# First FFN of a two-layer decoder: product in PSUM, table preparation in finer steps, first table loads issued by GpSimd

## The chip, the cores and the metric

The kernel runs on one core of a Trainium2 chip. The metric is device time in microseconds (us) of one execution. The engines are TensorE (PE, matrix products), VectorE (DVE), ScalarE (ACT), GpSimd (POOL) and SyncE (SP, which issues most DMAs). Each engine works through its own instructions in order and waits on semaphores for the others. SBUF is the on-chip memory; PSUM holds the results of PE in eight banks of 128 x 512 fp32.

## The reference

Two layers over x of 512 positions by 1024 channels, fp32: layer 0 has an attention mixer, layer 1 a diagonal state-space mixer (S5), and each is followed by the same kind of FFN. What the change touches is the FFN of layer 0 and, run beside it, the preparation of tables for the state-space layer.

```python
def conv_ffn(h, w_up, conv_w, conv_b, w_down):
    up = h @ w_up
    up = lax.conv_general_dilated(
        up, conv_w[:, None, :], window_strides=(1,), padding=[(CONV_W - 1, 0)],
        dimension_numbers=('NWC', 'WIO', 'NWC'), feature_group_count=2 * D_FF) + conv_b
    gate, val = jnp.split(up, 2, axis=-1)
    return (jax.nn.silu(gate) * val) @ w_down
...
    lam = lax.complex(a_re.astype(jnp.float32), a_im.astype(jnp.float32))
    lam_bar = jnp.exp(lam * dt)
    b_bar = ((lam_bar - 1) / lam)[..., None] * b_mat
```

D_FF is 2816, CONV_W is 3.

## The kernel before, in words

Every fp32 product is made of three matmuls with split operands (high times high, high times low, low times high; `mm3`, lines 169 to 173). A weight block `w_r` is loaded by SP (line 161), ACT rounds it to its high part `w_h` (L163), and DVE subtracts to get the low part `w_l` (L164). Three raw blocks and five split ones fit at a time.

The FFN has 22 units of 128 gate and 128 value channels, in groups of 8, 8 and 6. A unit takes two up products (`up_i_0` gate, `up_i_1` value; 24 matmuls of 128x512 each, one PSUM bank each). `unit_out` then works on them: `conv` (ACT L457 reads the bank and writes `ca` in SBUF, two DVE steps L459 add the other taps), Silu of the gate (ACT L466, in place), the product `gm` (DVE L469), its high part `gH` (ACT L473) and low part `gL` (DVE L474). The up products of the next units run on PE meanwhile. After each group come eight down products `dn_g_m` over the group's `gH` and `gL`. The PSUM pool `mm` has six banks handed out in turn, `aux` has two. The FFN of layer 1 uses the same function.

Beside the first FFN runs `ssm_prep`, a generator that computes the tables ("maps") of the state-space layer: powers and factors (`pw`, `fr`, `fi`, `lf`) on DVE and POOL, a recursion `tb` on POOL that is stored to `sR`, and then eight blocks. A block loads `lam` (from `sL`), `bt` and `bc`, makes `bl` and `cl` by complex products on POOL (`cmul`, L870 to 875, and L1073 to 1078), has PE multiply `cl` with `bd` into the small bank `pk` (L1017, in `direct`), makes `kz` of it, and stores `sB`, `sC` and `sT` by SP. `ball` is a table of the same kind as `bt`, loaded once before the blocks.

The order: the generator is written in steps (`yield`). `pace(us)` is called with 11.0 after each unit and 5.4 after each down product and takes one step for each `PACE` us; what a step writes stands in each engine's queue between the FFN's own instructions. `follow` chains the FFN's instructions on an engine, `held` keeps a DMA in program order on SP. `wg` are weight rows of the conditioning layer, loaded by SP and reduced on DVE (L196) between the rest.

Of the kernel before, what the change touches and what calls it, by code (L numbers as in the profile page):

```python
# [16 lines left out]
P = 128  # L17
# [24 lines left out]
BGU = 2  # L42
PACE = 12.0
NHOLD = 2
# [46 lines left out]
def _trunk(ctx, tc, I, out, tap):  # L91
# [47 lines left out]
    def follow(eng, fn):  # L139
        with tc.issue_after(line[eng].ins) if eng in line else ExitStack():  # L140
            line[eng] = fn()
        return line[eng]
# [281 lines left out]
    def ffn(l, R, prep=None, last=None, hook=lambda: None):  # L424
# [4 lines left out]
        with ExitStack() as fc:  # L429
# [33 lines left out]
            def unit_out(i, j, pss, nxt=lambda: None):  # L463
                cg = conv(i, 0, pss[0])
                nxt()
                follow("S", lambda: S.activation(cg, cg, AF.Silu))  # L466
                cv = conv(i, 1, pss[1])
                m = fp.tile([P, T], F32, tag="gm", bufs=1, name="gm")
                follow("V", lambda: V.tensor_tensor(m, cg, cv, ALU.mult))  # L469
                nxt()  # L470
                gh = fp.tile([P, T], F32R, tag=f"gH{j}", name=f"gH{i}")
                gl = fp.tile([P, T], F32R, tag=f"gL{j}", name=f"gL{i}")
                follow("S", lambda: S.activation(gh, m, AF.Copy))  # L473
                follow("V", lambda: V.tensor_tensor(gl, m, gh.bitcast(F32), ALU.subtract))  # L474
                return gh, gl
# [389 lines left out]
    def ssm_prep(fc):  # L865
# [14 lines left out]
        def gen():  # L880
# [30 lines left out]
            expo(mag, ph)  # L911
            yield

            V.tensor_tensor(ph, aim, dt, ALU.mult)
# [43 lines left out]
            V.tensor_tensor(fi, fi, den, ALU.mult)  # L958
            yield

            lf = pt_.tile([P, 2, 8, NPAIR], F32, tag="lf", name="lf")
            lt1, lt2 = (pt_.tile([P, 8, NPAIR], F32, tag=g, name=g) for g in ("lt1", "lt2"))
            f0, f1 = (f.rearrange("p (o q) -> p o q", o=1).to_broadcast([P, 8, NPAIR]) for f in (fr, fi))
            cmul(lf[:, 0, ::-1, :], lf[:, 1, ::-1, :], pw[:, 0, :8, :], pw[:, 1, :8, :], f0, f1, lt1, lt2)
            yield

# [10 lines left out]
            for hb in range(2):  # L977
# [5 lines left out]
                for q in range(6):  # L983
                    n = 1 << q
                    e0, e1 = bcast(co[:, 3 + q, ps_], n), bcast(si[:, 3 + q, ps_], n)
                    cmul(tb[:, 0, :, n:2 * n], tb[:, 1, :, n:2 * n], tb[:, 0, :, :n], tb[:, 1, :, :n], e0, e1, tt[:, 0, :, :n], tt[:, 1, :, :n])
                    if q > 3:
                        yield
                    if hb == 0 and q == 4:
                        lf_out()  # L990
# [14 lines left out]
            for ri in range(2):  # L1005
                SP.dma_start(ball[:, ri].rearrange("p a b -> p (a b)"), I[("b_re", "b_im")[ri]])

            def v3(t):
                return t[:, :512].rearrange("p (q o) -> p q o", o=16)

            cmul(bb[:, 0], bb[:, 1], ball[:, 0], ball[:, 1], bcast(fr, 16), bcast(fi, 16), v3(t1), v3(t2))

            def direct(bi, bd, cl):
# [6 lines left out]
                V.scalar_tensor_tensor(kz[:, 112:128], delta, sm("d_skip", bi, 1), kz[:, 112:128], ALU.mult, ALU.add)  # L1020
                for j in range(8):
                    SP.dma_start(sT[bi].rearrange("(h j) g c -> j g h c", j=8)[j], kz[:, 112 - 16 * j:240 - 16 * j])

            def held(out, in_):
                tc.keep_in_program_order(SP.dma_start(out, in_))

            def load_bl(bi):
                lam = pb.tile([P, 2, 512], F32, tag="lam", name="lam")
                bt = pb.tile([P, 2, 512], F32, tag="bt", name="bt")
                cs = slice(bi * 512, (bi + 1) * 512)  # L1030
                for ri in range(2):
                    held(lam[:, ri, :], sL[ri, :, cs].rearrange("(o j) x -> o j x", o=1).to_broadcast([16, 8, 512]))
                    held(bt[:, ri, :], I[("b_reT", "b_imT")[ri]][:, cs].rearrange("h (o x) -> h o x", o=1).to_broadcast([16, 8, 512]))
                return lam, bt
# [10 lines left out]
            for bi in range(8):  # L1045
                qs = slice(bi * 4, bi * 4 + 4)
                if owe:
                    cl_out(bi - 1, owe[2])
                bc = pb.tile([P, 2, 4, 16], F32, tag="bc", name="bc")
                for ri in range(2):  # L1050
                    held(bc[:, ri].rearrange("p a b -> p (a b)"), I[("c_re", "c_im")[ri]][:, bi * 64:(bi + 1) * 64])
                bl = pb.tile([P, 2, 512], F32, tag="bl", name="bl")
                lam, bt = nxt
                cmul(bl[:, 0], bl[:, 1], lam[:, 0], lam[:, 1], bt[:, 0], bt[:, 1], t1[:, :512], t2[:, :512])
                yield
                held(sB[bi].rearrange("p r n -> p (r n)"), bl.rearrange("p r n -> p (r n)"))
                if bi < 7:
                    nxt = load_bl(bi + 1)
                if owe:
                    direct(*owe)  # L1060
                cl = pb.tile([P, 2, 4, 9, 16], F32, tag="cl", name="cl")

# [17 lines left out]
                for g2 in range(2):  # L1080
                    rr = slice(g2 * 64, g2 * 64 + 64)
                    E.tensor_copy(bd[rr, :, :, g2 * 16:g2 * 16 + 16], bb[rr, :, qs, :])
                owe = bi, bd, cl
                yield
            cl_out(7, owe[2])
            direct(*owe)
            tc2.close()

# [407 lines left out]
```

## Time and profile before

| | |
|---|---|
| time, median of 3 runs | 1196.93 us (1194.94 to 1197.47) |
| profiled execution | 1194.65 us, its span 1192.7 us, mean granted clock 0.991 |
| PE busy | 1168.8 us (98%), 6218 matmuls |
| DVE busy | 885.8 us (74%) |
| ACT busy | 563.7 us (47%) |
| POOL busy | 270.4 us (23%) |

The first FFN takes the span from about 268 to 650 us, POOL's preparation 317 to 601 us of it. A timeline row gives the start in us, the duration in us, the engine, the line and the operation, and in brackets the idle time just before it and what ended it. A row of the line groups ends with count, busy us, mean ns of one, and idle before. A row of the waits gives the sum in us, the number of times and the longest. A row of windows gives the length, then busy time and count of PE, weight loads, DVE, ACT and POOL, the granted clock of PE, the DMA share and GB/s. A matmul record is longer than its share of PE's time, since matmuls overlap: distances between starts are read instead.

### The profile page before, as it was taken

How to read it: one execution, taken by the hardware profiler on the slowest of the kernel's cores; microseconds unless marked ns; L12 is line 12 of the kernel's file. 1: busy time of each engine (PE TensorE's matmuls, PEld its weight loads, DVE VectorE, ACT ScalarE, POOL GpSimd, SP SyncE). 2: the span in 40 equal slices, each digit the busy share in tenths (PEclk: the TensorE clock that was granted, in tenths of full speed). 3: DMA queues.
4: the chain of work that ended last, by engine and by line, in shares of the span. 5: the costliest groups of instructions: out<-in, count | busy, mean ns of one | idle time of the engine just before them, and what ended most of it. 6: DMA issues, size and time to landing. Idle time of an engine off the chain costs nothing.

```text
span 1192.7 us, 16459 instructions
## 1 busy us (share of the span) xinstructions
PE 1168.8 (98%) x6218; PEld 964.4 (81%) x6218; DVE 885.8 (74%) x1312; ACT 563.7 (47%) x893; POOL 270.4 (23%) x245
## 2 busy tenths in 40 slices
PE   8999999999999999989999999999999999999997
PEld 6887677699787878768889887879888888888887
DVE  6978988565999489888868598787598467744555
ACT  6756667456443134413336577646554134422443
POOL 1000000000298899998710000000000000000003
PEclk8999999999999999989999999999999999999999
DMA  8875653231348567778755598762166437442222
GB/s 301 316 262 165 203 179 109 90 121 54 89 142 273 177 215 222 207 233 294 247 153 182 182 322 288 246 224 77 53 216 225 124 118 188 153 124 71 83 76 71
DMA packets 92002, 211.00 MB, mean 177 GB/s; under 512 B 19602, under 2 KB 37906, under 8 KB 91923
## 3 DMA queue, kind: packets, MB, share of 16 engines
q1 hardware_dynamic: 83026, 205.76, 53.9%
q10 hardware_dynamic: 8320, 2.10, 0.8%
q0 software_dynamic: 576, 2.10, 0.5%
q8 instruction: 48, 0.79, 0.3%
q14 instruction: 32, 0.25, 0.1%
HBM read 188.68 MB, written 21.24 MB: 176 GB/s over the span
## 4 chain that ended last, share of the span: by engine, by line
PE 70%; POOL 8%; DVE 8%; DMA 7%; ACT 3%; issue 2%; SPq 1%; POOLq 0%; ACTq 0%; DVEq 0%
PE up L169 9%; PE up L172 9%; PE up L173 9%; PE dn L172 5%; PE dn L169 5%; PE dn L173 5%; PE o L772 2%; DVE ca L459 1%; PE t L754 1%; PE k L169 1%; PE q L169 1%; PE wo L169 1%; PE q L172 1%; PE q L173 1%; PE wo L173 1%
## 5 line engine op out<-in xcount | busy, mean ns | idle before, releaser
L173 PE MATMUL up<-hH,up_l 128*128 128x512 f32 x640 | 249.3, 390 | 1.1 <-DVE up_l L164 1.1
L169 PE MATMUL up<-hH,up_h 128*128 128x512 f32 x640 | 249.5, 390 | 0.0
L172 PE MATMUL up<-hL,up_h 128*128 128x512 f32 x640 | 249.3, 390 | 0.0
L459 DVE SCALAR_TENSOR_TENSOR ca<-up,small,ca 128x511 f32<-128x511 f32 (+1 forms) x176 | 131.4, 746 | 84.2 <-ACT ca L457 81.4
L196 DVE SCALAR_TENSOR_TENSOR wg<-wg,cact 128x1024 f32<-128x1024 f32 x96 | 122.8, 1294 | 40.1 <-DMA wg<-in_w_modT_dram 39.9
L172 PE MATMUL dn<-gL,dn_h 128*128 128x512 f32 (+1 forms) x394 | 145.9, 370 | 3.4 <-DVE gL L474 3.4
L169 PE MATMUL dn<-gH,dn_h 128*128 128x512 f32 (+1 forms) x394 | 146.3, 372 | 2.1 <-ACT gH L473 2.1
L173 PE MATMUL dn<-gH,dn_l 128*128 128x512 f32 (+1 forms) x394 | 145.7, 370 | 0.0
L173 PEld LDWEIGHTS up<-hH,up_l 128*128 128x128 f32 x640 | 120.1, 188 | 26.9 <-DVE up_l L164 2.0
L169 PEld LDWEIGHTS up<-hH,up_h 128*128 128x128 f32 x640 | 120.1, 188 | 26.0 <-issue 1.2
L172 PEld LDWEIGHTS up<-hL,up_h 128*128 128x128 f32 x640 | 120.1, 188 | 24.4
L1368 POOL TENSOR_SCALAR xa<-x,Anorm_out 128x256 f32<-128x256 f32 x7 | 5.7, 815 | 573.7 <-ACT dn_h L163 558.9
L163 ACT ACTIVATE up_h<-up_r 128x1024 fp32r<-128x1024 f32 x80 | 84.2, 1053 | 104.7 <-PE dn L172 48.0
L164 DVE TENSOR_TENSOR up_l<-up_r,up_h 128x1024 fp32r<-128x1024 f32 x80 | 121.9, 1524 | 10.1 <-ACT up_h L163 9.2
L457 ACT ACTIVATE ca<-up,small 128x512 f32<-128x512 f32 x88 | 67.7, 770 | 90.3 <-PE up L173 90.3
L172 PEld LDWEIGHTS dn<-gL,dn_h 128*128 128x128 f32 x394 | 75.1, 191 | 16.3 <-DVE gL L474 4.0
L169 PEld LDWEIGHTS dn<-gH,dn_h 128*128 128x128 f32 x394 | 75.0, 190 | 15.9 <-ACT gH L473 3.0
L173 PEld LDWEIGHTS dn<-gH,dn_l 128*128 128x128 f32 x394 | 75.0, 190 | 12.4
L353 DVE SCALAR_TENSOR_TENSOR x<-dn,mod,x 128x512 f32<-128x512 f32 (+1 forms) x55 | 37.3, 679 | 61.6 <-PE dn L173 61.6
L163 ACT ACTIVATE dn_h<-dn_r 128x1024 fp32r<-128x1024 f32 (+1 forms) x48 | 46.7, 981 | 55.9 <-PE dn L172 28.0
L466 ACT ACTIVATE ca<-ca 128x512 f32<-128x512 f32 x44 | 27.8, 632 | 91.7 <-DVE ca L459 89.9
L164 DVE TENSOR_TENSOR dn_l<-dn_r,dn_h 128x1024 fp32r<-128x1024 f32 (+1 forms) x48 | 62.8, 1308 | 8.3 <-ACT dn_h L163 8.1
(324 smaller groups left out, 2352.2 us busy)
## 6 DMA issues: line engine op xcount, KB each, us to landing
wg<-in_w_modT_dram SPq DMA_DIRECT2D x96, 512.0 KB
up_r<-in_w_up_dram SPq DMA_DIRECT2D x80, 512.0 KB
dn_r<-in_w_down_dram SPq DMA_DIRECT2D x32, 512.0 KB
wgs<-in_w_modT_dram SPq DMA_DIRECT2D x16, 512.0 KB
dn_r<-in_w_down_dram SPq DMA_DIRECT2D x16, 384.0 KB
wv_r<-in_w_v_dram SPq DMA_DIRECT2D x8, 512.0 KB
wk_r<-in_w_qk_dram SPq DMA_DIRECT2D x8, 512.0 KB
wq_r<-in_w_qk_dram SPq DMA_DIRECT2D x8, 512.0 KB
```

The source lines that it names most:

```text
L163: order("S", lambda: S.activation(wh[:, :n], raw[:, :n], AF.Copy))
L164: pin["split"] = order("V", lambda: V.tensor_tensor(wl[:, :n], raw[:, :n], wh[:, :n].bitcast(F32), ALU.subtract))
L169: ins = PE.matmul(ps, ah, bh, start=start, stop=False)
L172: PE.matmul(ps, ah, bl, start=False, stop=False)
L173: PE.matmul(ps, al, bh, start=False, stop=stop)
L196: mul = lambda: V.scalar_tensor_tensor(w, w, 1.0, cact, ALU.mult, ALU.mult, accum_out=raw[:, col:col + 1])
L353: add = lambda: V.scalar_tensor_tensor(xs, pv, gate, xs, ALU.mult, ALU.add)
L457: follow("S", lambda: S.activation(ca, ps, AF.Identity, bias=small[:, cb:cb + 1], scale=tapw[2]))
L459: follow("V", lambda: V.scalar_tensor_tensor(ca[:, q:], ps[:, :T - q], tapw[2 - q], ca[:, q:], ALU.mult, ALU.add))
L466: follow("S", lambda: S.activation(cg, cg, AF.Silu))
L754: ins = PE.transpose(pt[:, c:c + P], wts[pr][h2][i][:, j * P:(j + 1) * P], ident)
L772: ins = PE.matmul(po[pr][h2 * HD:(h2 + 1) * HD, j * P:], vn[:, j, hd:hd + HD], src, start=j == 0, stop=j == 3)
```

## The change

In the FFN of layer 0 (where `prep` is given) a PSUM bank takes the place of the SBUF tile `gm`: Silu writes the gate into it, DVE multiplies it by the value in place, and `gH` and `gL` are made from it. The bank comes from `aux` for units 0 and 1 and from `mm` for the others, so a unit then takes three of the six. In FFN 1 nothing is changed. `PACE` is 6 instead of 12; the steps of the first part are doubled (an empty one after each), three empty steps stand ahead of the first block, and a block has four steps instead of two: `bl`; then the former block's `sC` store and `pk`, and the load of `bc`; then `cl` and four of the former block's `sT` stores; then the store of `bl`, the next loads and the other four. The loads of `ball` and the first `lam` and `bt`, six DMAs, are issued by GpSimd (`G`) instead of SP.

```diff
-PACE = 12.0
+PACE = 6.0
@@ -463,10 +463,12 @@
             def unit_out(i, j, pss, nxt=lambda: None):
                 cg = conv(i, 0, pss[0])
                 nxt()
-                follow("S", lambda: S.activation(cg, cg, AF.Silu))
+
+                m = bank(aux if i < 2 else mm, "gm") if prep else fp.tile([P, T], F32, tag="gm", bufs=1, name="gm")
+                ga = m if prep else cg
+                follow("S", lambda: S.activation(ga, cg, AF.Silu))
                 cv = conv(i, 1, pss[1])
-                m = fp.tile([P, T], F32, tag="gm", bufs=1, name="gm")
-                follow("V", lambda: V.tensor_tensor(m, cg, cv, ALU.mult))
+                follow("V", lambda: V.tensor_tensor(m, ga, cv, ALU.mult))
                 nxt()
                 gh = fp.tile([P, T], F32R, tag=f"gH{j}", name=f"gH{i}")
                 gl = fp.tile([P, T], F32R, tag=f"gL{j}", name=f"gL{i}")
@@ -910,6 +912,7 @@
             expo(mag, ph)
             yield
+            yield
...
@@ -986,6 +991,7 @@
                     cmul(tb[:, 0, :, n:2 * n], tb[:, 1, :, n:2 * n], tb[:, 0, :, :n], tb[:, 1, :, :n], e0, e1, tt[:, 0, :, :n], tt[:, 1, :, :n])
                     if q > 3:
                         yield
+                        yield
                     if hb == 0 and q == 4:
                         lf_out()
                 for ri in range(2):
@@ -1003,12 +1009,16 @@
             bb = pb.tile([P, 2, NPAIR, 16], F32, tag="bb", name="bb")
             ball = pb.tile([P, 2, NPAIR, 16], F32, tag="bl", name="ball")
             for ri in range(2):
-                SP.dma_start(ball[:, ri].rearrange("p a b -> p (a b)"), I[("b_re", "b_im")[ri]])
+                G.dma_start(ball[:, ri].rearrange("p a b -> p (a b)"), I[("b_re", "b_im")[ri]])
 
             def v3(t):
                 return t[:, :512].rearrange("p (q o) -> p q o", o=16)
 
             cmul(bb[:, 0], bb[:, 1], ball[:, 0], ball[:, 1], bcast(fr, 16), bcast(fi, 16), v3(t1), v3(t2))
+
+            yield
+            yield
+            yield
 
             def direct(bi, bd, cl):
                 pk = bank(aux, f"pk{bi}")
@@ -1018,19 +1028,24 @@
                 kz = kza[:, bi % 2, :]
                 S.activation(kz[:, 112:], pk[:, :P], AF.Copy)
                 V.scalar_tensor_tensor(kz[:, 112:128], delta, sm("d_skip", bi, 1), kz[:, 112:128], ALU.mult, ALU.add)
-                for j in range(8):
-                    SP.dma_start(sT[bi].rearrange("(h j) g c -> j g h c", j=8)[j], kz[:, 112 - 16 * j:240 - 16 * j])
+
+            def t_out(bi, js):
+                kz = kza[:, bi % 2, :]
+                for j in js:
+                    held(sT[bi].rearrange("(h j) g c -> j g h c", j=8)[j], kz[:, 112 - 16 * j:240 - 16 * j])
 
             def held(out, in_):
                 tc.keep_in_program_order(SP.dma_start(out, in_))
 
+
             def load_bl(bi):
+                put = held if bi else G.dma_start
                 lam = pb.tile([P, 2, 512], F32, tag="lam", name="lam")
                 bt = pb.tile([P, 2, 512], F32, tag="bt", name="bt")
                 cs = slice(bi * 512, (bi + 1) * 512)
                 for ri in range(2):
-                    held(lam[:, ri, :], sL[ri, :, cs].rearrange("(o j) x -> o j x", o=1).to_broadcast([16, 8, 512]))
-                    held(bt[:, ri, :], I[("b_reT", "b_imT")[ri]][:, cs].rearrange("h (o x) -> h o x", o=1).to_broadcast([16, 8, 512]))
+                    put(lam[:, ri, :], sL[ri, :, cs].rearrange("(o j) x -> o j x", o=1).to_broadcast([16, 8, 512]))
+                    put(bt[:, ri, :], I[("b_reT", "b_imT")[ri]][:, cs].rearrange("h (o x) -> h o x", o=1).to_broadcast([16, 8, 512]))
                 return lam, bt
 
             def cl_out(bi, cl):
@@ -1044,20 +1059,17 @@
             nxt = load_bl(0)
             for bi in range(8):
                 qs = slice(bi * 4, bi * 4 + 4)
-                if owe:
-                    cl_out(bi - 1, owe[2])
-                bc = pb.tile([P, 2, 4, 16], F32, tag="bc", name="bc")
-                for ri in range(2):
-                    held(bc[:, ri].rearrange("p a b -> p (a b)"), I[("c_re", "c_im")[ri]][:, bi * 64:(bi + 1) * 64])
                 bl = pb.tile([P, 2, 512], F32, tag="bl", name="bl")
                 lam, bt = nxt
                 cmul(bl[:, 0], bl[:, 1], lam[:, 0], lam[:, 1], bt[:, 0], bt[:, 1], t1[:, :512], t2[:, :512])
                 yield
-                held(sB[bi].rearrange("p r n -> p (r n)"), bl.rearrange("p r n -> p (r n)"))
-                if bi < 7:
-                    nxt = load_bl(bi + 1)
                 if owe:
+                    cl_out(bi - 1, owe[2])
                     direct(*owe)
+                bc = pb.tile([P, 2, 4, 16], F32, tag="bc", name="bc")
+                for ri in range(2):
+                    held(bc[:, ri].rearrange("p a b -> p (a b)"), I[("c_re", "c_im")[ri]][:, bi * 64:(bi + 1) * 64])
+                yield
                 cl = pb.tile([P, 2, 4, 9, 16], F32, tag="cl", name="cl")
 
                 def v4(t):
@@ -1080,10 +1092,19 @@
                 for g2 in range(2):
                     rr = slice(g2 * 64, g2 * 64 + 64)
                     E.tensor_copy(bd[rr, :, :, g2 * 16:g2 * 16 + 16], bb[rr, :, qs, :])
+                if owe:
+                    t_out(bi - 1, range(4))
                 owe = bi, bd, cl
+                yield
+                held(sB[bi].rearrange("p r n -> p (r n)"), bl.rearrange("p r n -> p (r n)"))
+                if bi < 7:
+                    nxt = load_bl(bi + 1)
+                if bi:
+                    t_out(bi - 1, range(4, 8))
                 yield
             cl_out(7, owe[2])
             direct(*owe)
+            t_out(7, range(8))
             tc2.close()
 
         g = gen()
```

What it moves shows best at three places. The first is DVE in group 0, from unit 3's convolution (`ca` from `up_3_0`) to the split of `up_5_0`; `pw`, `mag`, `ft`, `lr`, `fr`, `fi` are small 128x32 tables of the preparation. Before:

```order
L934 TENSOR_TENSOR pw<-mag,si 128x32
L459 SCALAR_TENSOR_TENSOR ca_3046<-up_3_0_2996,small,ca_3046 128x511
L934 TENSOR_TENSOR pw<-mag,co 128x32
L952 TENSOR_TENSOR ft_3264<-pw,small 128x32
L459 SCALAR_TENSOR_TENSOR ca_3046<-up_3_0_2996,small,ca_3046 128x510
L164 TENSOR_TENSOR up_5_0_l<-up_5_0_r,up_5_0_h 128x1024
L936 TENSOR_TENSOR mag<-mag 128x32
L945 TENSOR_SCALAR lr<-pw 128x32
L934 TENSOR_TENSOR pw<-mag,co 128x32
L934 TENSOR_TENSOR pw<-mag,si 128x32
L459 SCALAR_TENSOR_TENSOR ca_3057<-up_3_1_3021,small,ca_3057 128x511
```

Now (above these rows stand eight more of the same kind, `pw`, `pw`, `ft`, `mag`, `lr`, `pw`, `pw`, `ft`, and nothing of the FFN):

```order
L939 TENSOR_TENSOR mag<-mag 128x32
L956 TENSOR_TENSOR fr<-ft_3182,ft_3183 128x32
L937 TENSOR_TENSOR pw<-mag,co 128x32
L937 TENSOR_TENSOR pw<-mag,si 128x32
L957 TENSOR_TENSOR fr<-fr,den 128x32
L958 TENSOR_TENSOR ft_3182<-pw,small 128x32
L959 TENSOR_TENSOR ft_3183<-lr,small 128x32
L459 SCALAR_TENSOR_TENSOR ca_3097<-up_3_0_3047,small,ca_3097 128x511
L939 TENSOR_TENSOR mag<-mag 128x32
L960 TENSOR_TENSOR fi<-ft_3182,ft_3183 128x32
L459 SCALAR_TENSOR_TENSOR ca_3097<-up_3_0_3047,small,ca_3097 128x510
L164 TENSOR_TENSOR up_5_0_l<-up_5_0_r,up_5_0_h 128x1024
```

Small operations that followed the split stand before the convolution and the split now. The second place is SP behind the load of `up_9_0`, early among group 1's weights. Before:

```order
L161 DMA up_9_0_r<-in_w_up_dram 128x1024
L1006 DMA ball<-in_b_re_dram 128x512
L1006 DMA ball<-in_b_im_dram 128x512
L1025 DMA lam<-sL 128x1x512
L195 DMA wg_3825<-in_w_modT_dram 128x1024
L1025 DMA bt<-in_b_reT_dram 128x1x512
L1025 DMA lam<-sL 128x1x512
L1025 DMA bt<-in_b_imT_dram 128x1x512
L1025 DMA bc<-in_c_re_dram 128x64
L1025 DMA bc<-in_c_im_dram 128x64
L161 DMA up_9_1_r<-in_w_up_dram 128x1024
L195 DMA wg_3898<-in_w_modT_dram 128x1024
```

Now SP at the same place, and then POOL from the clearing of `bd` to the first product of `ball`:

```order
L161 DMA up_9_0_r<-in_w_up_dram 128x1024
L195 DMA wg_3847<-in_w_modT_dram 128x1024
L161 DMA up_9_1_r<-in_w_up_dram 128x1024
L195 DMA wg_3882<-in_w_modT_dram 128x1024
L161 DMA up_10_0_r<-in_w_up_dram 128x1024
L195 DMA wg_3917<-in_w_modT_dram 128x1024
L161 DMA up_10_1_r<-in_w_up_dram 128x1024
L1038 DMA bc<-in_c_re_dram 128x64
L1038 DMA bc<-in_c_im_dram 128x64
```

```order
L1006 MEMSET bd 128x512
L1012 DMA ball<-in_b_re_dram 128x512
L1012 DMA ball<-in_b_im_dram 128x512
L1047 DMA lam<-sL 128x1x512
L1048 DMA bt<-in_b_reT_dram 128x1x512
L1047 DMA lam<-sL 128x1x512
L1048 DMA bt<-in_b_imT_dram 128x1x512
L872 TENSOR_TENSOR t_3803<-ball,fr 128x512
```

The six loads left SP for POOL's queue, and `bc` stands behind three more weight loads of the FFN. The third place is SP around the load of `dn_1_2`, the third down weight of group 1. Before:

```order
L161 DMA dn_1_0_r<-in_w_down_dram 128x1024
L161 DMA dn_1_1_r<-in_w_down_dram 128x1024
L1025 DMA sB<-bl 128x1024
L1025 DMA lam<-sL 128x1x512
L1025 DMA bt<-in_b_reT_dram 128x1x512
L1025 DMA lam<-sL 128x1x512
L1025 DMA bt<-in_b_imT_dram 128x1x512
L161 DMA dn_1_2_r<-in_w_down_dram 128x1024
```

Now:

```order
L161 DMA dn_1_0_r<-in_w_down_dram 128x1024
L161 DMA dn_1_1_r<-in_w_down_dram 128x1024
L1038 DMA sC<-cl 256x1x128 x4
L1038 DMA bc<-in_c_re_dram 128x64
L1038 DMA bc<-in_c_im_dram 128x64
L161 DMA dn_1_2_r<-in_w_down_dram 128x1024
L1038 DMA sB<-bl 128x1024
L1038 DMA lam<-sL 128x1x512
```

The store of `bl` and the block's loads, which stood ahead of `dn_1_2`, stand behind it, and stores of `cl` ahead of it.

More of the change, by code (lines that the diff above doesn't have):

```diff
@@ L1055, in gen @@
                 yield
-                held(sB[bi].rearrange("p r n -> p (r n)"), bl.rearrange("p r n -> p (r n)"))
-                if bi < 7:
-                    nxt = load_bl(bi + 1)
                 if owe:
+                    cl_out(bi - 1, owe[2])
                     direct(*owe)
+                bc = pb.tile([P, 2, 4, 16], F32, tag="bc", name="bc")
+                for ri in range(2):
+                    held(bc[:, ri].rearrange("p a b -> p (a b)"), I[("c_re", "c_im")[ri]][:, bi * 64:(bi + 1) * 64])
+                yield
                 cl = pb.tile([P, 2, 4, 9, 16], F32, tag="cl", name="cl")
@@ L1082, in gen @@
                     E.tensor_copy(bd[rr, :, :, g2 * 16:g2 * 16 + 16], bb[rr, :, qs, :])
+                if owe:
+                    t_out(bi - 1, range(4))
                 owe = bi, bd, cl
+                yield
+                held(sB[bi].rearrange("p r n -> p (r n)"), bl.rearrange("p r n -> p (r n)"))
[3 more added lines that the diff above has]
+                    t_out(bi - 1, range(4, 8))
                 yield
```

## The prediction

> **What bounds the kernel now.** I read the page first: the engine totals, the forty slices, the chain that ended last.
>
> ```profile
> PE 1168.8 (98%) x6218; PEld 964.4 (81%) x6218; DVE 885.8 (74%) x1312; ACT 563.7 (47%) x893; POOL 270.4 (23%) x245
> PE   8999999999999999989999999999999999999997
> DVE  6978988565999489888868598787598467744555
> PE 70%; POOL 8%; DVE 8%; DMA 7%; ACT 3%; issue 2%; SPq 1%; POOLq 0%; ACTq 0%; DVEq 0%
> ```
>
> PE is busy for 98% of the span, so time can only be won where PE waits, or runs slowly after a wait. A slice is 29.8 us; the first FFN is slices 10 to 22, where DVE stands at 8 and 9. Next I read PE's waits, then the timeline at each of them.
>
> ```profile
> PE dn L172 <- DVE gL L474: 3.4, 2, 2.7
> PE dn L169 <- ACT gH L473: 2.1, 2, 1.1
> PE up L173 <- DVE up_l L164: 1.1, 2, 0.9
> ...
> 311.83 0.39 PE L169 MATMUL up<-hH,up_h 128*128 128x512 f32 x1
> 314.10 0.39 PE L172 MATMUL up<-hL,up_h 128*128 128x512 f32 x1
> 315.39 0.50 PE L173 MATMUL up<-hH,up_l 128*128 128x512 f32 x1 [0.90 <-DVE up_l L164]
> ...
> 368.36 0.39 PE L173 MATMUL dn<-gH,dn_l 128*128 128x512 f32 x1
> 369.76 0.49 PE L169 MATMUL dn<-gH,dn_h 128*128 128x512 f32 x1 [1.01 <-ACT gH L473]
> 370.95 0.50 PE L172 MATMUL dn<-gL,dn_h 128*128 128x512 f32 x1 [0.69 <-DVE gL L474]
> 372.44 0.63 PE L169 MATMUL dn<-gH,dn_h 128*128 128x512 f32 x1
> 375.86 0.40 PE L169 MATMUL dn<-gH,dn_h 128*128 128x512 f32 x1
> ...
> 446.26 0.50 PE L173 MATMUL up<-hH,up_l 128*128 128x512 f32 x1 [0.25 <-DVE up_l L164]
> ...
> 505.88 0.39 PE L173 MATMUL dn<-gH,dn_l 128*128 128x512 f32 x1
> 507.40 0.50 PE L169 MATMUL dn<-gH,dn_h 128*128 128x512 f32 x1 [1.13 <-ACT gH L473]
> 510.62 0.80 PE L172 MATMUL dn<-gL,dn_h 128*128 128x512 f32 x1 [2.72 <-DVE gL L474]
> 515.89 0.40 PE L173 MATMUL dn<-gH,dn_l 128*128 128x512 f32 x1
> ```
>
> The first column is the start. From 311.83 to 314.10 there are ten steps, 0.227 us each: that is the undisturbed pace. Four places lose against it. At 314.1 one step takes 1.29, a loss of 1.1. At the first group boundary (up products to dn products) 16 matmuls start between 368.36 and 375.86, 7.50 us instead of 3.63: a loss of 3.9, of which only 1.7 is idle time; in the rest PE runs at half pace (0.63 records after the wait). At 446.26 it loses 0.3. At the second boundary 12 matmuls and one pk group (0.6) stand in 505.88 to 515.89, 10.01 us instead of 3.3: a loss of 6.7. Sum 12.0 us. That is what this change can win at most.
>
> **Term 1, the gate and the product in PSUM.** The line groups of DVE, with GpSimd at work (297 to 375 us) and in the second FFN without it (900 to 1080 us); the last number before the second bar is the mean in ns.
>
> ```profile
> L459 DVE SCALAR_TENSOR_TENSOR ca<-up,small,ca 128x510 f32<-128x510 f32 x16 | 11.9, 744 | 0.2
> L469 DVE TENSOR_TENSOR gm<-ca,ca 128x512 f32<-128x512 f32 x8 | 8.0, 1006 | 0.1
> L474 DVE TENSOR_TENSOR gL<-gm,gH 128x512 fp32r<-128x512 f32 x8 | 7.2, 897 | 0.0
> ...
> L459 DVE SCALAR_TENSOR_TENSOR ca<-up,small,ca 128x510 f32<-128x510 f32 x20 | 15.0, 749 | 0.6
> L469 DVE TENSOR_TENSOR gm<-ca,ca 128x512 f32<-128x512 f32 x10 | 6.9, 693 | 0.3
> L474 DVE TENSOR_TENSOR gL<-gm,gH 128x512 fp32r<-128x512 f32 x10 | 6.8, 685 | 0.0
> ...
> 300.00:400.00 100.00, 97.40 (x422) 79.53 (x422) 92.14 (x164) 38.90 (x52) 72.89 (x99) 0.98 0.49 156
> 900.00:1080.00 180.00, 180.00 (x796) 149.05 (x795) 112.53 (x145) 61.57 (x74) 0.00 (x0) 1.00 0.52 152
> ```
>
> The convolution step L459 has one input in PSUM and one in SBUF and costs 744 ns beside GpSimd and 749 without. The product and the residue gL, with both inputs in SBUF, cost 1006 and 897 beside it and 693 and 685 without. After the change both have one input in PSUM. I price them at L459's 744: nearest in operands and size. The 16 of group 0 then cost 11.9 us instead of 8.0 + 7.2 = 15.2: DVE wins 3.3 us, before the first boundary, where it is busy 92% of the time and PE waits for it. The price is no gain everywhere: in units 0 to 2, where GpSimd is still quiet, six operations become some 0.05 dearer (744 against 693), so the split that is late at 315.39 comes 0.2 to 0.3 later. No row shows DVE writing a product into PSUM; bounds are 0.69 (as in SBUF) and 1.5 (reading and writing paid one after the other, twice 744). ACT's Silu now writes PSUM and its copy reads PSUM; ACT is busy 39 of 100 us there and hides 0.1 us each.
>
> The bank count changes too: a unit takes three of the six banks, so an up product must wait for the convolution of two units back instead of three. A product is 24 matmuls, 5.45 us, so DVE may lag 16.4 us behind (three products) where it had 27. Whether that holds is seen at the tightest place, up_5_0, in the rows of term 2: the convolution of unit 3 that it will wait for had ended when DVE began the split at 323.07, and up_5_0's first matmul came two steps ahead of 326.42, at 325.97. That is 2.9 us of room, nearly all of which term 2 uses. I charge nothing beside the split's own wait there, and keep 2 us as the upper end of both.
>
> **Term 2, the small operations moved ahead of up_5_0's split.** On DVE 14 of them (128x32) now stand before the convolution of unit 3 and the split of up_5_0, which had been spread behind it.
>
> ```profile
> 323.07 1.21 DVE L164 TENSOR_TENSOR up_l<-up_r,up_h 128x1024 fp32r<-128x1024 f32 x1
> ...
> L934 DVE TENSOR_TENSOR pw<-mag,si x4: 198/308/440, 321.4 to 333.2; 128x32 f32<-128x32 f32 x4
> ...
> 326.42 0.39 PE L173 MATMUL up<-hH,up_l 128*128 128x512 f32 x1
> ```
>
> The fastest of a kind took 198 ns, so 14 cost 2.8 us (4.3 at the median 308). The split ended at 324.28 and will end at 327.1; PE asked for it at 326.42. I charge 0.8 (ends 0 and 2.3). The wait for the bank falls into the same time.
>
> **Boundary 1.** gL of unit 7 let PE go at 370.95. DVE does the same number of operations up to there and saves 3.3, so gL comes at 367.7; PE arrives 1.1 later than before (0.8 and 0.3), for the dn_h product that stood at 368.6, now 369.7. Two microseconds of slack: the 3.9 go, half pace included.
>
> **Term 3, the map loads leave SP.** SP's rows, and what hangs on them:
>
> ```profile
> 383.33 0.33 SPq L161 DMA_DIRECT2D up_r<-in_w_up_dram  x1
> 401.84 0.33 SPq L1006 DMA_DIRECT2D ball<-in_b_re_dram  x1
> ...
> 489.98 0.33 SPq L1025 DMA_DIRECT2D sB<-bl  x1
> 493.01 1.01 SPq L161 DMA_DIRECT2D dn_r<-in_w_down_dram  x2
> ...
> 502.10 1.52 DVE L164 TENSOR_TENSOR dn_l<-dn_r,dn_h 128x1024 fp32r<-128x1024 f32 x1 [3.65 <-ACT dn_h L163]
> ```
>
> SP stands at the load of ball from 383.7 to 401.8, with every later weight load queued behind it, and again at the store of bl until 490; the down weights of dn_1_2 leave only at 493 and DVE waits 3.65 us for their split at 502.1, with the product of unit 15 behind it. So the 6.7 at the second boundary are a late load first, and slow operations after it. Now ball and the first lam and bt loads stand on GpSimd's queue, and dn_1_2's load stands ahead of the bl store. Both waits leave the weights' path, and the product and gL of unit 15 lose their collisions too: I count 0.3 + 6.7 won. What is late next is no weight: raw tiles are three deep, so SP is held by splits, as in the second FFN, where PE was busy 180.00 of 180.00.
>
> **Term 4, what GpSimd pays.**
>
> ```profile
> 398.28 0.77 POOL L992 DMA_DIRECT2D sR<-tb  x1 [0.30 <-POOL tb L875]
> 404.53 1.05 POOL L870 TENSOR_TENSOR t<-ball,fr 128x512 f32<-128x512 f32 x1 [4.72 <-DMA ball<-in_b_re_dram]
> 434.41 2.29 POOL L1078 TENSOR_TENSOR cl<-t,t 128x576 f32<-128x576 f32 x1
> 439.21 0.64 PE L1017 MATMUL pk<-cl,bd 128*32 128x128 f32 x16
> ```
>
> Its own issue of a store took 0.77. Six loads are 4.6 us, from 401.8 when the stores of tb have landed (that is when SP got through): arithmetic from 406.4 instead of 404.5, 1.9 later. cl of block 0 ended at 436.7; PE takes it at pk0, 2.5 later. PE arrives there 3.9 earlier by boundary 1 and 1.1 later by the above: 436.4. GpSimd gains as DVE does from fewer collisions (0 to 3.3 by then), so cl comes between 435.3 and 438.6. I charge 1.0 (ends 0 and 2.2). Blocks after it have 20 us and more each against PE's 22 for two units. pk3, pk4 and pk7 stand one or two products later than before: nothing. The empty steps add no instruction. SP's store order changes, all behind loads that have their lead.
>
> **A rule against it.** The 0.77 us row is the trace's price. The Trainium skill, "SBUF — State Buffer", in its warning on the "DVE blocks DMA" trap, says that the descriptors of a DMA issued from GpSimd's queue are written by GpSimd, which cannot do so while DVE runs a two-port copy, and gives 3100 ns instead of 620 for such a DMA. By its figure six loads would take 18.6 us, an estimate, PE would wait some 15 us at pk0, and the sum would be about 1202. The row at 398.28, issued in the midst of DVE's stream, does not show it.
>
> **Sum.** 12.0 lost before; left are 1.4 (314), 0.8 (up_5_0), 1.0 (pk0) = 3.2. Gain 8.8. The profiled execution took 1194.65 us (span 1192.7), 2.3 below the median of 1196.93, and would come to 1185.9; on the median it is 1188.1, say 1188.0.
>
> **Rivals.** (a) Down weights still late, since SP now meets store after store between them (sC before dn_1_2, sT between dn_1_3 and dn_1_5): boundary 2 keeps half to all of its 6.7; gain 5.4 to 2.1, 1191.5 to 1194.8. For it: SP's 18 us stand shows how long a store can hold it. Against: dn_1_2 itself goes earlier. 14%. (b) The change does not end the collisions: a product that writes PSUM but reads one SBUF tile still costs 1006. Then boundary 1 keeps its 3.9, gain 4.9, 1192.0. Against: L459's 744. 8%. (c) DVE pays for PSUM twice, 1.5 us each, in units 0 to 7: 24.0 instead of 15.2, so PE, waiting for DVE there, loses 8.8 more, through the banks too; boundary 2 gives 7.0 back: 1198.7. From 1.54 us each (15.2 + 7.0 + 2.4, over 16) it is slower. For it: no row. 10%. (d) GpSimd's queue makes block 0 late: each microsecond of cl beyond 436.4 is one of PE at pk0. The gain without pk0 is 9.8; it is used up when cl comes at 446, and from 448.6 the kernel is slower: against the 437.4 of my sum, each of the six loads would have to take 1.9 us more than 0.77. At 3 us each (18 in all) cl comes at 450.8 and the time is 1201.5. 8%, for the row speaks against it.
>
> **Numbers.** Forecast 60%: 1188.0, its own range 1185 to 1190.5 (no new stall 1185.9, both at their upper ends 1190.6). 0.2% is 2.4 us, about what a measurement of this kernel can tell from no change. Faster: 60 + 8 of (b) + 11 of (a) = 79%. Same: 3 of (a), 5 of (c), 1 of (d) = 9%. Slower: 5 of (c), 7 of (d) = 12%. The range runs from 1184.8 (all 12.0 won on the median is 1184.9) to 1195.5, which takes in (a) and (b) and leaves out (c) and (d).
>
> **What would show it.** In the profile after: the product and gL of the first FFN near 745 ns in every stretch; no PE wait for gL or gH at the two boundaries, and none of the 0.63 records there; SP without an 18 us stand at a ball load; a wait under 1 us for up_5_0's split near 327; pk0 of PE after at most 2 us of waiting. Wrong if PE's up products wait for ca of two units back, if gm costs over 1 us, or if dn_1_2's split is still late.

## The result, and the profile after

The changed kernel took 1184.34 us (median of 4 runs, 1182.73 to 1185.38) against 1197.15 (1194.94 to 1197.47): ratio 0.990, 95% interval 0.9876 to 0.9923. The changed kernel is faster, by 12.8 us on these medians; the two profiled executions, 1194.65 and 1184.69, differ by 10.0. Measured again with the experiments it took 1184.82 against 1193.23 (23 runs, 1188.72 to 1197.92), ratio 0.9932 (0.9915 to 0.9948). The kernel before moves by several us from set to set, the changed one by less than one. One of the eleven runs of the last version below took 1710.87 us, at a granted clock of 0.635 where the others had 0.994 or more, and is left out of its median.

The gain lies in the first FFN. From its first up matmul to its last down matmul the two profiles of the kernel before have 374.7 and 372.5 us (the second stands among the experiments), those of the changed kernel 363.8 and 365.6.

The page after, the lines that answer to those of before:

```profile
PE 1164.3 (98%) x6218; PEld 961.8 (81%) x6218; DVE 856.5 (72%) x1312; ACT 564.9 (48%) x893; POOL 260.6 (22%) x251
PE   8999999999999999999999999999999999999997
DVE  6969888566899657787857588887598368744555
PE 80%; DVE 8%; DMA 6%; ACT 3%; issue 2%; POOL 0%; SPq 0%; POOLq 0%; ACTq 0%; DVEq 0%
```

DVE lost 29 us of work with the same number of instructions, and GpSimd left the chain that ended last (8% before, 0 now). The waits of PE between 260 and 640 us, and the timeline at the four places that had lost time:

```profile
PE stat L264 <- DVE acc L243: 0.9, 1, 0.9
PE up L173 <- DVE up_l L164: 0.3, 1, 0.3
PE up L169 <- DVE ca L459: 0.3, 1, 0.3
...
314.79 0.39 PE L173 MATMUL up<-hH,up_l 128*128 128x512 f32 x1
315.47 0.47 PE L169 MATMUL up<-hH,up_h 128*128 128x512 f32 x1 [0.29 <-DVE ca L459]
315.77 0.40 PE L172 MATMUL up<-hL,up_h 128*128 128x512 f32 x1
316.51 0.50 PE L173 MATMUL up<-hH,up_l 128*128 128x512 f32 x1 [0.34 <-DVE up_l L164]
...
369.72 0.39 PE L169 MATMUL dn<-gH,dn_h 128*128 128x512 f32 x1
369.95 0.39 PE L172 MATMUL dn<-gL,dn_h 128*128 128x512 f32 x1
...
502.80 0.39 PE L169 MATMUL dn<-gH,dn_h 128*128 128x512 f32 x1
503.03 0.39 PE L172 MATMUL dn<-gL,dn_h 128*128 128x512 f32 x1
```

Near 315 about 1.0 us is still lost, part of it now to the bank (up_4_0 waits for the convolution `ca` of unit 2). The other rows are the matmuls that waited for the last gH and gL of groups 0 and 1 before. Both group boundaries pass at the full pace of 0.227 us, with none of the 0.63 records. What DVE and GpSimd did there:

```profile
L471 DVE TENSOR_TENSOR gm<-gm,ca 128x512 f32<-128x512 f32 x8 | 5.6, 696 | 0.2
L476 DVE TENSOR_TENSOR gL<-gm,gH 128x512 fp32r<-128x512 f32 x8 | 5.4, 680 | 0.0
...
325.98 1.30 DVE L164 TENSOR_TENSOR up_l<-up_r,up_h 128x1024 fp32r<-128x1024 f32 x1
327.53 0.39 PE L173 MATMUL up<-hH,up_l 128*128 128x512 f32 x1
368.04 0.68 DVE L476 TENSOR_TENSOR gL<-gm,gH 128x512 fp32r<-128x512 f32 x1
498.64 0.68 DVE L476 TENSOR_TENSOR gL<-gm,gH 128x512 fp32r<-128x512 f32 x1
...
404.51 0.56 POOL L1012 DMA_DIRECT2D ball<-in_b_re_dram  x1 [4.60 <-DMA sR<-tb]
435.17 1.43 POOL L1090 TENSOR_TENSOR cl<-t,t 128x576 f32<-128x576 f32 x1
436.46 0.64 PE L1027 MATMUL pk<-cl,bd 128*32 128x128 f32 x16
```

Product and residue stand at 696 and 680 ns beside GpSimd (297 to 375 us; 1006 and 897 before). The last gL of group 0 ends at 368.7, that of group 1 at 499.3, 1.2 and 3.7 us before PE wants them. cl of block 0 ends just as PE arrives at pk0.

### The profile page after: what moved, and what is told of

Same layout as the page of the kernel before. It is cut to its first block, busy times and chain, and to the rows that moved or that the text cites. A ratio compares the mean times of both kernels' runs of the same rounds, so it can differ in the third digit from the quotient of the medians.

```text
span 1182.5 us, 16493 instructions
## 1 busy us (share of the span) xinstructions
PE 1164.3 (98%) x6218; PEld 961.8 (81%) x6218; DVE 856.5 (72%) x1312; ACT 564.9 (48%) x893; POOL 260.6 (22%) x251
## 4 chain that ended last, share of the span: by engine, by line
PE 80%; DVE 8%; DMA 6%; ACT 3%; issue 2%; POOL 0%; SPq 0%; POOLq 0%; ACTq 0%; DVEq 0%
PE up L169 13%; PE up L172 13%; PE up L173 13%; PE dn L169 6%; PE dn L172 6%; PE dn L173 6%; DMA wg<-in_w_modT_dram 3%; DVE om L744 2%; DVE wg L196 1%; PE v L169 1%; PE wo L169 1%; PE wo L173 1%; PE v L172 1%; PE v L173 1%; PE wo L172 1%
## 5 line engine op out<-in xcount | busy, mean ns | idle before, releaser
L459 DVE SCALAR_TENSOR_TENSOR ca<-up,small,ca 128x511 f32<-128x511 f32 (+1 forms) x176 | 131.6, 748 | 119.2 <-ACT ca L457 116.2
L196 DVE SCALAR_TENSOR_TENSOR wg<-wg,cact 128x1024 f32<-128x1024 f32 x96 | 120.3, 1267 | 24.1 <-DMA wg<-in_w_modT_dram 23.8
L164 DVE TENSOR_TENSOR up_l<-up_r,up_h 128x1024 fp32r<-128x1024 f32 x80 | 113.7, 1421 | 10.1 <-ACT up_h L163 9.1
L169 PEld LDWEIGHTS dn<-gH,dn_h 128*128 128x128 f32 x394 | 74.3, 188 | 12.8 <-issue 0.6
```

The lines of the kernel that those rows point to most:

```text
L164: pin["split"] = order("V", lambda: V.tensor_tensor(wl[:, :n], raw[:, :n], wh[:, :n].bitcast(F32), ALU.subtract))
L169: ins = PE.matmul(ps, ah, bh, start=start, stop=False)
L196: mul = lambda: V.scalar_tensor_tensor(w, w, 1.0, cact, ALU.mult, ALU.mult, accum_out=raw[:, col:col + 1])
L459: follow("V", lambda: V.scalar_tensor_tensor(ca[:, q:], ps[:, :T - q], tapw[2 - q], ca[:, q:], ALU.mult, ALU.add))
```

## The experiments

Two theories stood at the start. A: boundary 1 was lost to collisions of two-SBUF-input operations with GpSimd, boundary 2 first of all to weights that waited in SP's queue. B: the collisions were all.

**The PSUM tiles alone.** The edit to the kernel before:

```diff
-                follow("S", lambda: S.activation(cg, cg, AF.Silu))
...
-                m = fp.tile([P, T], F32, tag="gm", bufs=1, name="gm")
+                m = bank(aux if i < 2 else mm, "gm") if prep else fp.tile([P, T], F32, tag="gm", bufs=1, name="gm")
+                ga = m if prep else cg
+                follow("S", lambda: S.activation(ga, cg, AF.Silu))
```

> The kernel before with the gate and product in PSUM, and nothing else of the change. Theory A (boundary 1 is lost to collisions of DVE's two-SBUF-input operations with GpSimd, boundary 2 first of all to a late down weight): product and gL near 0.69 us everywhere, boundary 1 without a wait (3.9 us won), the split of dn_1_2 still late behind the store of bl, so boundary 2 keeps 5 us or more: gain 3 to 5 us, about 1193. Theory B (all comes from the collisions): both boundaries go, gain 9 to 12, about 1186.

It was slower: 1197.68 against 1194.64, ratio 1.0038 (1.0024 to 1.0053). Neither theory had that. The profile shows both boundaries without a wait, as B wants (the second with PE 9.5 us later by then), and a new loss between them: SP's queue, DVE and PE of this kernel.

```profile
368.90 0.34 SPq L161 DMA_DIRECT2D dn_r<-in_w_down_dram  x1
393.88 0.33 SPq L1007 DMA_DIRECT2D ball<-in_b_re_dram  x1
...
398.06 1.23 DVE L196 SCALAR_TENSOR_TENSOR wg<-wg,cact 128x1024 f32<-128x1024 f32 x1 [22.52 <-DMA wg<-in_w_modT_dram]
...
401.34 0.79 PE L173 MATMUL dn<-gH,dn_l 128*128 128x512 f32 x1 [7.03 <-DVE dn_l L164]
401.93 0.63 PE L169 MATMUL dn<-gH,dn_h 128*128 128x512 f32 x1
410.92 0.60 PE L173 MATMUL dn<-gH,dn_l 128*128 128x512 f32 x1 [2.45 <-DVE dn_l L164]
```

The scheduler that writes the queues set the load of ball ahead of the load of dn_0_7 here, four weights earlier than before. It waits for the stores of tb, SP stands for 25 us, and DVE stands at a wg whose load is behind it. PE waits first for the split of dn_0_6, which stands behind that wg on DVE though its weights had been loaded, and then for the split of dn_0_7.

**The order alone**: the changed kernel with gate and product back in SBUF.

```diff
-                m = bank(aux if i < 2 else mm, "gm") if prep else fp.tile([P, T], F32, tag="gm", bufs=1, name="gm")
-                ga = m if prep else cg
-                follow("S", lambda: S.activation(ga, cg, AF.Silu))
+                follow("S", lambda: S.activation(cg, cg, AF.Silu))
...
+                m = fp.tile([P, T], F32, tag="gm", bufs=1, name="gm")
```

> The changed kernel with gate and product in SBUF as before: the steps, the store order and the loads on GpSimd alone. Theory A: boundary 2 is gone (6 to 7 us won), boundary 1 stays (3 to 4 us lost) and the split of up_5_0 may be late by 1: gain 5 to 7, about 1191. Theory B: gm and gL at 1.0 to 1.6 us keep DVE late at both boundaries, gain under 2, about 1196.

Ratio 0.9999 (0.9985 to 1.0013): no gain. SP does not stand at ball (its longest for a DMA of the preparation is 10.2 us, at a store of bl) and both boundaries are clean, but PE waits for something else, the transposes of lf, which the new steps put ahead of up_7_0. This kernel first, then the changed one:

```profile
353.11 0.72 POOL L876 TENSOR_TENSOR lf<-lt,lt 128x256 f32<-128x256 f32 x1
353.88 0.69 PE L974 MATMUL ptl<-consts,lf 128*128 128x128 f32 x2 [5.97 <-POOL lf L876]
```

```profile
343.86 0.73 POOL L877 TENSOR_TENSOR lf<-lt,lt 128x256 f32<-128x256 f32 x1
348.86 0.60 PE L975 MATMUL ptl<-consts,lf 128*128 128x128 f32 x4
```

In the changed kernel lf is ready 9 us earlier, 4 us ahead of PE. The cause lies in DVE's queue: in this kernel the small tables stand behind up_5_0's split, as in the kernel before, and the last of them (`fi`) is made at 334.7; in the changed kernel they stand ahead of it and `fi` is made at 327.6. The run with four tiles from aux, below, has the PSUM tiles and lf as late as here, so it is this order that makes lf late. The collisions may add some 2 us: from `fi` to lf it takes 18.8 us here and 16.2 there, and PE waits 6.0 here and 3.3 there. That boundary 1 is clean here says nothing against the collisions. The last gL of group 0 ends at 372.6; without the 6.0 us at lf, PE would have wanted it near 371.1.

**Only the gate in PSUM**, in the kernel before: the product reads it there but writes SBUF, and gL reads two SBUF tiles.

```diff
-                follow("S", lambda: S.activation(cg, cg, AF.Silu))
+                ga = bank(aux if i < 2 else mm, "ga") if prep else cg
+                follow("S", lambda: S.activation(ga, cg, AF.Silu))
...
-                follow("V", lambda: V.tensor_tensor(m, cg, cv, ALU.mult))
+                follow("V", lambda: V.tensor_tensor(m, ga, cv, ALU.mult))
```

> The kernel before with only the gate in PSUM: the product reads one PSUM and one SBUF tile and writes SBUF, gL still has both inputs in SBUF. Theory A (the number of SBUF inputs decides): product at 0.69 us with and without GpSimd, gL at 0.9 in group 0 and 1.6 in group 1 as before; gain 1 to 2.5, about 1195. Theory B (an SBUF output collides as well): the product stays at 1.0 or more and the time at 1197.

1197.3, ratio 1.0034 (1.0016 to 1.0053); it has the early ball load and SP's stand like the PSUM tiles alone, so its time says nothing of the tiles. Its operations do (420 to 506 us; this kernel, then the kernel before):

```profile
L475 DVE TENSOR_TENSOR gL<-gm,gH 128x512 fp32r<-128x512 f32 x7 | 12.2, 1739 | 0.0
L470 DVE TENSOR_TENSOR gm<-ga,ca 128x512 f32<-128x512 f32 x7 | 4.8, 689 | 0.1
```

```profile
L474 DVE TENSOR_TENSOR gL<-gm,gH 128x512 fp32r<-128x512 f32 x7 | 11.6, 1651 | 0.0
L469 DVE TENSOR_TENSOR gm<-ca,ca 128x512 f32<-128x512 f32 x8 | 9.9, 1244 | 0.2
```

One input moved to PSUM frees the product of the collision, whatever it writes to; gL with two SBUF inputs keeps it. That part of theory A is shown.

**The loads back on SP**, else the changed kernel.

```diff
-                G.dma_start(ball[:, ri].rearrange("p a b -> p (a b)"), I[("b_re", "b_im")[ri]])
+                SP.dma_start(ball[:, ri].rearrange("p a b -> p (a b)"), I[("b_re", "b_im")[ri]])
...
-                put = held if bi else G.dma_start
+                put = held
```

> The changed kernel with ball and the first lam and bt loads back on SP. Theory A (the order of dn_1_2's load ahead of the bl store does the work at boundary 2, and DVE now has slack for a late weight in group 1): SP stands 10 to 18 us at the ball load, DVE waits for a wg or a split, PE loses under 2 us: 1184 to 1186. Theory B (the loads on GpSimd are what frees SP): the loss of 6 us or part of it comes back, 1188 or more.

1197.65 against 1194.64, ratio 1.0041 (1.0025 to 1.0056): the whole gain is gone. That is theory B's 1188 or more, but twice the 6 us that it named. SP stood from 367 to 392 at ball, once more ahead of dn_0_7:

```profile
391.95 0.33 SPq L1012 DMA_DIRECT2D ball<-in_b_re_dram  x1
...
402.37 0.80 PE L173 MATMUL dn<-gH,dn_l 128*128 128x512 f32 x1 [10.01 <-DVE dn_l L164]
```

A new theory C: what counts is that no DMA that waits stands ahead of a weight in SP's queue; each part of the change removes one such stand or exposes another. The second set tells it from "GpSimd's queue is what helps".

**PSUM tiles and loads on GpSimd, steps as before**: the first edit and the reverse of the last, in the kernel before.

```diff
+                m = bank(aux if i < 2 else mm, "gm") if prep else fp.tile([P, T], F32, tag="gm", bufs=1, name="gm")
...
+                G.dma_start(ball[:, ri].rearrange("p a b -> p (a b)"), I[("b_re", "b_im")[ri]])
+                put = held if bi else G.dma_start
```

> The kernel before with the PSUM tiles and the six loads on GpSimd, the steps as before. Theory A (a load that waits for the stores of tb must not stand in SP's queue ahead of dn_0_7; that is what the PSUM tiles alone lacked): no 22 us stand of SP, no PE wait at dn_0_7, boundaries 1 and 2 clean; a rest of 0 to 5 us, since the store of bl now stands ahead of up_10_1: 1183 to 1189. Theory B (the finer steps are needed as well): SP stands as long at bc or at the store of bl, PE waits 6 us or more in group 1: 1192 or more.

1190.9 against 1194.56, ratio 0.9964 (0.995 to 0.9979), between the two. The next waiting DMA took the place of ball: the store of bl, ahead of up_10_1.

```profile
SPq L1026 <- POOL bl L876: 50.7, 8, 27.5
...
434.21 0.50 PE L169 MATMUL up<-hH,up_h 128*128 128x512 f32 x1 [2.86 <-ACT up_h L163]
436.06 0.79 PE L173 MATMUL up<-hH,up_l 128*128 128x512 f32 x1 [1.04 <-DVE up_l L164]
```

**The loads on GpSimd alone**, in the kernel before (the lines with G of the last diff).

> The kernel before with nothing but the six loads on GpSimd. Theory A: DVE's 14 us wait for wg goes; boundary 1 stays at 3 to 4 us (collisions), boundary 2 shrinks to 2 to 5: 1190 to 1193 where before is 1195. Theory B (the loads matter only with the PSUM tiles): within 1 us of before.

Ratio 1.0009 (0.9991 to 1.0027): theory B's figure, but not for its reason. SP again stood at the store of bl, boundary 1 lost 1.2 us, boundary 2 kept its wait, and PE waited at pk0:

```profile
SPq L1025 <- POOL bl L875: 50.9, 6, 25.4
...
PE dn L172 <- DVE gL L474: 3.3, 2, 2.7
PE pk L1017 <- POOL cl L1079: 2.7, 1, 2.7
```

This run and the one before it differ in the PSUM tiles alone. In both the store of bl stands ahead of dn_1_2, as in the kernel before. SP issues the loads of dn_1_2 and dn_1_3 behind it, with the tiles and then without:

```profile
487.13 1.01 SPq L161 DMA_DIRECT2D dn_r<-in_w_down_dram  x2
```

```profile
497.21 1.01 SPq L161 DMA_DIRECT2D dn_r<-in_w_down_dram  x2
```

With the tiles bl is made sooner, the loads leave 10 us earlier, DVE no longer waits for the split of dn_1_2 (1.9 us without), and the last gL of group 1 has 4.3 us in hand. So the tiles alone ended the late load here. `fi` is made 8.9 us sooner with them; what share of the 10 us this order has, and what share GpSimd's fewer collisions, was not separated.

**The loads on SP, but later**: the changed kernel with the three empty steps moved ahead of the load of ball, which puts it behind up_10_0.

```diff
+            yield
+            yield
+            yield
             ball = pb.tile([P, 2, NPAIR, 16], F32, tag="bl", name="ball")
...
-                G.dma_start(ball[:, ri].rearrange("p a b -> p (a b)"), I[("b_re", "b_im")[ri]])
+                held(ball[:, ri].rearrange("p a b -> p (a b)"), I[("b_re", "b_im")[ri]])
```

> The changed kernel with ball and the first lam and bt on SP again, but behind up_10_0 and not ahead of dn_0_7 (the three empty steps stand ahead of them). Theory A (the place in the queue decides, not the queue): SP stands under 6 us at ball, PE waits under 2 us in group 1, at pk0 if anywhere: 1183 to 1187. Theory B (GpSimd's queue itself is what helps): 1190 or more.

1183.57 against 1194.56, ratio 0.9898 (0.988 to 0.9917): as fast as the change, without GpSimd's queue. It is the place in the queue. (The load of ball is also held in program order here.) SP still stands for the stores of tb, under 7 us:

```profile
396.14 0.33 SPq L195 DMA_DIRECT2D wg<-in_w_modT_dram  x1
403.02 0.33 SPq L1010 DMA_DIRECT2D ball<-in_b_re_dram  x1
```

cl of block 0 is ready at 434.5 and pk0 at 437.6, 3 us in hand where the changed kernel has none.

**The kernel before, profiled again.**

> The kernel before once more, for a second profile. If the losses are fixed by the program, the boundaries lose 3.9 and 6.7 us again to within 1, and the ratio is 1; if they hang on how the DMAs fall, one of them differs by 2 us or more.

Ratio 0.9985 (0.997 to 1.0001). The losses are not fixed: boundary 1 lost some 1.1 us and boundary 2 this:

```profile
511.83 0.39 PE L169 MATMUL dn<-gH,dn_h 128*128 128x512 f32 x1
513.29 0.50 PE L172 MATMUL dn<-gL,dn_h 128*128 128x512 f32 x1 [1.07 <-DVE gL L474]
```

Some 1.3 us, and no half pace behind it; instead there are steps of 1.1, 1.6 and 1.4 us at high and low parts of weights near 418 and 448, the last two followed by eight matmuls at half pace. SP stood at ball for 18.5 us again. Which product waits differs from one execution to the next.

**The changed kernel again**, in the last set.

> The changed kernel once more, on the chip of this set. 1182 to 1186, with no PE wait over 0.5 us in the first FFN but the two near 315.

1184.82; its one difference is at pk0:

```profile
PE pk L1027 <- POOL cl L1090: 1.7, 1, 1.7
```

**Without the three empty steps.**

```diff
-            yield
-            yield
-            yield
 
             def direct(bi, bd, cl):
```

> The changed kernel without the three empty steps ahead of the first block: pk0 then stands on PE ahead of up_9_0, at 415, and the store of bl on SP ahead of up_11_0. Theory A (the empty steps put PE's and SP's waits where GpSimd's results are there): cl of block 0 still comes at 434 to 437, PE waits some 20 us at pk0, 1200 to 1207. Theory B (they are only there for order, and GpSimd's work comes earlier too): 1183 to 1187.

1201.93 against 1193.23, ratio 1.0073 (1.0055 to 1.0091): theory A's time, with a shorter wait. cl came at 431.2, a little earlier, and PE waited 11.8 us for its first part and 3.3 for its second.

```profile
427.30 0.66 PE L1023 MATMUL pk<-cl,bd 128*32 128x128 f32 x8 [11.83 <-POOL cl L1083]
```

**Four product tiles from aux**, the changed kernel with one number.

```diff
-                m = bank(aux if i < 2 else mm, "gm") if prep else fp.tile([P, T], F32, tag="gm", bufs=1, name="gm")
+                m = bank(aux if i < 4 else mm, "gm") if prep else fp.tile([P, T], F32, tag="gm", bufs=1, name="gm")
```

> The changed kernel with the product tiles of units 2 and 3 in aux too, so that up_4_0 need not wait for the convolution of unit 2. Theory A (the bank rule costs next to nothing, since DVE is late for the split of up_4_0 in the same place): the bank wait of 0.3 at 315 goes, the wait for the split grows by as much; the time of the changed kernel to within 1 us. Theory B (three banks a unit tie PE to DVE in group 0): 1 to 3 us faster than the changed kernel.

1189.73, ratio 0.9974 (0.9962 to 0.9986) where the changed kernel beside it had 0.9932: 5 us slower than it, and neither theory. The bank wait went and the split wait took its place, as A has it. But the scheduler put the small tables behind up_5_0's split again, and lf came late:

```profile
352.41 0.72 POOL L877 TENSOR_TENSOR lf<-lt,lt 128x256 f32<-128x256 f32 x1
353.18 0.44 PE L975 MATMUL ptl<-consts,lf 128*128 128x128 f32 x2 [3.32 <-POOL lf L877]
```

`fi` is made at 336.5 here. The small operations that the prediction charged as a delay are what brings lf in time for its transposes, and the bank of gate and product is what makes the scheduler put them there. In every run whose units 2 and 3 take it from mm, `fi` is finished 58.5 or 58.6 us after the first up matmul, also with the steps as before; in every other run it takes 67.0 to 68.0. So the tiles moved these operations, not the finer steps. That the scheduler acts on the wait of up_4_0 for a bank is inferred.

**Later loads on SP with four tiles from aux.**

> The loads on SP behind up_10_0, and the product tiles of units 2 and 3 in aux: the version that the runs so far point to. 1182 to 1185 if the two do not touch each other, no PE wait over 1 us in the first FFN; 1187 or more if aux is then taken when the transposes of lf or pk0 need it.

1189.8 (median of ten runs), ratio 0.9963 (0.9949 to 0.9977), with the same 3.3 us at ptl. No version here is shown to beat the changed kernel: the one with the later loads on SP equals it within the spread of its two sets (0.990 and 0.9932 against 0.9898).

## Why the prediction was right, point by point

The time came out at the lower end of the range, 3.7 us below the forecast. The first median, 1184.34, lies 0.5 below the range's end of 1184.8 and the second, 1184.82, on it; the ratio of 0.990 on the 1196.93 of the forecast gives 1185.0. The first median gain of 12.8 is above the forecast 8.8, the second of 8.4 below it. One figure of the range is off: with no new stall the sum gives 1186.3 (1.4 of the 12.0 left), not 1185.9.

- What could be won. Right in kind: PE lost its time at these four places. But the 12.0 were read from one execution as if fixed. The second profile of before has 2.4 us where this had 10.6 at the boundaries, and other losses elsewhere.
- Term 1. Right in mechanism, the price 50 to 60 ns too high: 696 and 680 instead of 744. L459 was the wrong neighbour; PSUM cost nothing visible (693 and 685 in SBUF without GpSimd). DVE won 15.2 - 11.0 = 4.2 instead of 3.3. ACT's Silu and copy, charged with 0.1 us more each, took 602 and 600 ns instead of 633 and 633. GpSimd won too, as allowed for: from the first product of ball to the end of cl it took 32.2 us before (404.5 to 436.7) and 27.9 now (408.7 to 436.6).
- 314: 1.0 instead of 1.4. The bank wait that I charged at nothing beside the split is 0.3 of it, and it falls on up_4_0, not on up_5_0, which I took for the tightest place. It is a wait for `ca` of two units back, one of the signs that I had named for being wrong; it costs only 0.3 us.
- Term 2: 0 instead of 0.8. The split ended at 327.3 as worked out (327.1), but PE, later since the start of the FFN, asked at 327.5: 0.2 of slack. That the transposes of lf, moved ahead of up_7_0, need just this order, I did not see: the prediction has no term for their move, and that it cost nothing was luck.
- Boundary 1: gone, as said, with 1.2 us in hand instead of 2: the last gL ended at 368.7, not 367.7. Without the tiles it lost 1.1 to 3.9 us in each of the three profiles in which PE had not been held by lf before it; with them it lost nothing in any.
- Term 3: boundary 2 gone. That the loads of dn_1_2 left late in the kernel before was read rightly. That they had to pass the store of bl was not: with the tiles and the loads on GpSimd the store stays ahead of them, and the boundary is clean. No run has the tiles and late loads of dn_1_2 together, so the shares of load and collisions in the 6.7 stay open. That the place of a stand is set by the scheduler and moves with an edit elsewhere I did not say; rival (a), stores held in front of weights, is what the partial versions ran into.
- Term 4: 0 in one profile and 1.7 in the other, for 1.0 (0 to 2.2). Its parts were off in opposite directions: GpSimd stood 4.6 for the stores, until 404.5 and not 401.8, and issued six loads in 0.56 each, 3.2 in all, not 4.6; the first product then waited 0.9 for ball to land. Rival (d) did not come. The Trainium skill, "SBUF — State Buffer", in the warning on the "DVE blocks DMA" trap, has the descriptors of such a DMA held up while DVE runs a two-port copy. The trace does not test it: while GpSimd issued, from 404.5 to 407.8, DVE ended one wg reduction at 405.8 and then stood idle until 410.2.
- The terms do not add. Alone, the tiles cost 3.0 us more on the medians, and neither the loads nor the order (steps and loads together) gave anything; all together they bring 8 to 13. The sum came out because nearly all of PE's waits in the first FFN went at once.

## What to carry to other kernels

An in-order queue that issues weights should hold no DMA ahead of them that waits for a slow producer for longer than the weights' lead. (SP of the changed kernel still stands 14.0 us at a store of bl, until 427.7, and no PE wait follows.) Read each queue's stands first, then ask where the scheduler will put that DMA after the edit, since it moves. A part of a change that shows no gain alone may still be needed: look which wait took over before it is dropped. Where a scheduler sets the order, compare the orders of two variants before a difference in time is put down to the edit itself.

## What the runs showed of the hardware

With one input in PSUM, a 128x512 product took 689 ns beside GpSimd where it wrote SBUF and 696 where it wrote PSUM; with two inputs in SBUF product and residue took 1244 and 1651 in group 1. The Trainium skill, "SBUF — State Buffer", section "SBUF: two separate sides", gives a lock on a shared port pair for it; the traces agree.

Half pace after a wait is a granted clock of 0.50 in these traces (372.1 to 374.9 us in the kernel before, 354.2 to 357.2 in the one with four tiles). After the 3.3 us at ptl in that kernel:

```profile
354.65 0.63 PE L172 MATMUL up<-hL,up_h 128*128 128x512 f32 x1
355.08 0.63 PE L173 MATMUL up<-hH,up_l 128*128 128x512 f32 x1
```

It is not set by the idle time alone: 1.7 us idle in two pieces (1.0 and 0.7) at boundary 1 of before was followed by it, 1.7 us in one piece at pk0 in the second profile of the changed kernel was not. Every single wait of PE of 2.4 us or more in the first FFN of these runs was followed by it. The Trainium skill, "TensorE: Matmul & The Clock Gate", section "What's actually happening", has a free-running window of 3.4 us, which would let the outcome hang on where the wait falls. The shortest single wait with half pace behind it, 2.45 us, is shorter than that window; no run here was made to test where it fell.
